# Pairing the x loads and grouping the stores of an eight-expert MLP, with fifteen small reads issued by SP

## The chip, the cores and the metric

The kernel runs on one core of a Trainium2 chip. The metric is the device time of one execution in microseconds (us); the kernel before was run five times, with a median of 184.09 us (183.85 to 184.23). A sixth execution was taken by the hardware profiler, and all durations below come from it.

## The reference

Eight experts each apply a two-layer MLP to their own 256 rows. All inputs and the output are float32.

```python
n_experts, capacity, hidden, expert_hidden = 8, 256, 512, 2048
# x: (8, 256, 512)   w1: (8, 512, 2048)   w2: (8, 2048, 512)
h = np.matmul(x, w1)
h = np.maximum(h, 0)
return np.matmul(h, w2).astype(np.float32)
```

One w1 and one w2 of an expert are 4 MB each in memory, one x is 512 KB and one output 512 KB. Everything together is 71.3 MB read and 4.2 MB written.

## The kernel before, in words

The loads cast from float32 to bfloat16 on the way, so they are all issued by POOL (`load_x`, line 66; `load_w1`, line 70; `load_w2`, line 74); only the x of experts 0 and 1 comes through SP in float32 and is cast by DVE (`load_x_first`, line 60). POOL also issues the stores of experts 0 to 6 (`store`, line 84). The last expert's two output halves are stored by SP and ACT (lines 160 to 162).

Per expert e: `prepare` (line 104) transposes x on PE through PSUM and DVE copies it to `xT`. `layer1` (line 117) makes `hT`, 64 matmuls of 256 columns with a Relu on ACT after every eight. `layer2` (line 139) makes the output, 32 matmuls of 512 columns into two PSUM banks, which DVE copies to `out_sb` (for the last expert, ACT copies the second half).

The order of PE's and POOL's instructions is the order in which the program writes them (`tc.manual_schedule`, line 166). POOL's order is that of `loads` (lines 89 to 94): for each expert x, w1, w2, with w1 of expert 7 ahead of w2 of expert 6. In iteration e of the main loop `issue` (line 96) takes from that list what may be issued by then (line 173), and `store(e - 1)` follows (line 175). The stores of experts 4, 5 and 6 (`DEFER`, line 56) are issued after the loop, behind all the loads.

w2 is loaded whole for experts 0 to 5, in three pieces of 8, 4 and 4 row blocks for expert 6, and in seven pieces of 4, 4, 3, 2, 1, 1, 1 for expert 7 (`PIECES`, line 53). A row block is 128 rows of w2: 256 KB in memory, and two matmuls of `layer2`. For the two experts with pieces `layer2` goes through the blocks in the outer loop, so that it can begin with the first piece.

POOL issues 37 transfers: 8 of w1, 16 of w2, 6 of x, 7 stores. Their completion semaphores go round: in the trace each transfer of POOL carries the semaphore of the one eight places earlier, and waits until that one has landed. So at most eight are in flight. Besides, a load waits for its buffer: w1 has four buffers, the whole w2 three, x four.

Of the kernel before, what the change touches and what calls it, by code (L numbers as in the profile page):

```python
# [9 lines left out]
FP32 = mybir.dt.float32  # L10
BF16 = mybir.dt.bfloat16


@with_exitstack
def kernel(
    ctx: ExitStack,
    tc: tile.TileContext,
    x: bass.AP,
    w1: bass.AP,
    w2: bass.AP,  # L20
    out: bass.AP,
):
    nc = tc.nc
    P = 128
    E, C, H = x.shape
    F = w1.shape[2]
    MC = C // P
    K1 = H // P
    K2 = F // P

    x_v = x.rearrange("e (p mo) k -> e p (mo k)", mo=MC)
    out_v = out.rearrange("e (p mo) k -> e p (mo k)", mo=MC)
    w1_v = w1.rearrange("e (p ko) n -> e p (ko n)", ko=K1)
    w2_v = w2.rearrange("e (p j) n -> e p (j n)", p=P)

    const = ctx.enter_context(tc.tile_pool(name="const", bufs=1))
    x_pool = ctx.enter_context(tc.tile_pool(name="x_pool", bufs=2))
    xb_pool = ctx.enter_context(tc.tile_pool(name="xb_pool", bufs=4))  # L40
    xT_pool = ctx.enter_context(tc.tile_pool(name="xT_pool", bufs=2))
    w1_pool = ctx.enter_context(tc.tile_pool(name="w1_pool", bufs=4))
    w2_pool = ctx.enter_context(tc.tile_pool(name="w2_pool", bufs=1))
    hT_pool = ctx.enter_context(tc.tile_pool(name="hT_pool", bufs=2))
    out_pool = ctx.enter_context(tc.tile_pool(name="out_pool", bufs=5))
    psum_t = ctx.enter_context(tc.tile_pool(name="psum_t", bufs=1, space=bass.MemoryType.PSUM))
    psum_h = ctx.enter_context(tc.tile_pool(name="psum_h", bufs=3, space=bass.MemoryType.PSUM))
    psum_o = ctx.enter_context(tc.tile_pool(name="psum_o", bufs=4, space=bass.MemoryType.PSUM))

    identity = const.tile([P, P], BF16, name="identity")  # L50


    PIECES = {E - 2: [8, 4, 4], E - 1: [4, 4, 3, 2, 1, 1, 1]}
    BUFS = {16: 3, 8: 1, 4: 4, 3: 1, 2: 1, 1: 3}

    DEFER = (E - 4, E - 3, E - 2)

    xbs, w1s, w2s, outs = {}, {}, {}, {}

    def load_x_first(e):  # L60
        t = x_pool.tile([P, MC * H], FP32, name="x_sb")
        nc.sync.dma_start(t[:], x_v[e])
        xbs[e] = xb_pool.tile([P, MC, P, K1], BF16, name="xb")
        nc.vector.tensor_copy(xbs[e][:].rearrange("p m q k -> p (m q k)"), t[:])  # L64

    def load_x(e):
        xbs[e] = xb_pool.tile([P, MC, P, K1], BF16, name="xb")
        nc.gpsimd.dma_start(xbs[e][:].rearrange("p m q k -> p (m q k)"), x_v[e])  # L68

    def load_w1(e):  # L70
        w1s[e] = w1_pool.tile([P, K1 * F], BF16, name="w1_sb")
        nc.gpsimd.dma_start(w1s[e][:], w1_v[e])  # L72

    def load_w2(e):
        w2s[e] = []
        k = 0
        for n in PIECES.get(e, [16]):
            c = w2_pool.tile([P, n * H], BF16, name=f"w2_{n}", bufs=BUFS[n])
            nc.gpsimd.dma_start(c[:], w2_v[e, :, k * H:(k + n) * H])  # L79
            for q in range(n):  # L80
                w2s[e].append(c[:, q * H:(q + 1) * H])
            k += n

    def store(e):
        nc.gpsimd.dma_start(out_v[e], outs[e][:].rearrange("p m h -> p (m h)"))  # L85

    loads = []
    for e in range(E):  # L90
        if e + 1 < E and e >= 1:
            loads.append((load_x, e + 1))
        loads += [(load_w1, e), (load_w2, e)]
    loads[-3], loads[-2] = loads[-2], loads[-3]

    def issue(upto):
        while loads:
            f, e = loads[0]
            if (f, e) not in upto:
                break  # L100
            loads.pop(0)
            f(e)

    def prepare(e):
        xb = xbs[e]
        xt_ps = psum_t.tile([P, K1, MC, P], BF16, name="xt_ps")
        for ko in range(K1):
            for mo in range(MC):
                nc.tensor.transpose(xt_ps[:, ko, mo, :], xb[:, mo, :, ko], identity[:])  # L109
        xT = xT_pool.tile([P, K1, C], BF16, name="xT")  # L110
        nc.vector.tensor_copy(  # L111
            xT[:].rearrange("p k c -> p (k c)"),
            xt_ps[:].rearrange("p k m q -> p (k m q)"),
        )
        return xT

    def layer1(e, xT):
        w1_r = w1s[e][:].rearrange("p (ko q j) -> p ko q j", ko=K1, j=K2)
        hT = hT_pool.tile([P, K2, C], BF16, name="hT")
        for pr in range(K2 // 2):  # L120
            h_ps = psum_h.tile([P, 2, C], FP32, name="h_ps")
            for s in range(2):
                j = pr * 2 + s
                for ko in range(K1):
                    nc.tensor.matmul(  # L125
                        h_ps[:, s, :],
                        w1_r[:, ko, :, j],
                        xT[:, ko, :],
                        start=(ko == 0),
                        stop=(ko == K1 - 1),  # L130
                    )
            nc.scalar.activation(  # L132
                hT[:, pr * 2:pr * 2 + 2, :].rearrange("p a c -> p (a c)"),
                h_ps[:].rearrange("p a c -> p (a c)"),
                mybir.ActivationFunctionType.Relu,
            )
        return hT

    def layer2(e, hT):
        last = e == E - 1  # L140
        out_sb = outs[e] = out_pool.tile([P, MC, H], FP32, name="out_sb")
        o_ps = [psum_o.tile([P, H], FP32, name="o_ps") for _ in range(MC)]
        if e in PIECES:
            order = [(k, m) for k in range(K2) for m in range(MC)]
        else:
            order = [(k, m) for m in range(MC) for k in range(K2)]
        for k, m in order:
            nc.tensor.matmul(  # L148
                o_ps[m][:],
                hT[:, k, m * P:(m + 1) * P],  # L150
                w2s[e][k],
                start=(k == 0),
                stop=(k == K2 - 1),
            )
            if k == K2 - 1:
                if last and m == 1:
                    nc.scalar.copy(out_sb[:, m, :], o_ps[m][:])  # L157
                else:
                    nc.vector.tensor_copy(out_sb[:, m, :], o_ps[m][:])  # L159
                if last:  # L160
                    eng = nc.scalar if m == 1 else nc.sync
                    eng.dma_start(out_v[e, :, m * H:(m + 1) * H], out_sb[:, m, :])

    load_x_first(0)
    load_x_first(1)
    with tc.manual_schedule(engines={mybir.EngineType.PE, mybir.EngineType.Pool}):
        f, e = loads.pop(0)
        f(e)
        make_identity(nc, identity)
        issue([(load_w2, 0), (load_x, 2), (load_w1, 1), (load_w2, 1), (load_x, 3), (load_w1, 2)])  # L170
        xT = prepare(0)
        for e in range(E - 1):
            issue([(load_w2, e + 2), (load_x, e + 4), (load_w1, e + 3), (load_w1, E - 1), (load_w2, e + 1)])
            if e > 0 and e - 1 not in DEFER:
                store(e - 1)
            hT = layer1(e, xT)
            xT = prepare(e + 1)
            if e == E - 2:
                hT_last = layer1(E - 1, xT)
            layer2(e, hT)  # L180
        for e in DEFER:
            store(e)
        layer2(E - 1, hT_last)


# [1 line left out]
_INS = ['x', 'w1', 'w2']  # L187
_OUTS = [((8, 256, 512), 'float32')]
# [25 lines left out]
```

## Time and profile before

| what | value |
|---|---|
| median of five runs | 184.09 us |
| the profiled execution, its own time | 183.88 us |
| its span, from the first to the last instruction | 182.1 us |
| PE busy | 128.3 us (70%) |
| POOL busy, 43 instructions | 20.8 us (11%) |
| POOL's transfers (queue q0), share of the 16 DMA engines' time | 97.6% |
| SP's and ACT's transfers (q1, q10) | 1.9% and 0.4% |
| HBM read and written | 71.30 MB and 4.19 MB |

A row of a timeline has the start and the duration in us, the engine, the line, the operation, what it writes and reads, and in brackets how long the engine had been idle and what ended that. "POOL" with an operation DMA_DIRECT2D is POOL writing the descriptors of one transfer; the transfer itself runs later on the 16 DMA engines. "Landing" is the moment when all 16 engines have raised the transfer's semaphore.

### The profile page before, as it was taken

To read this page: it belongs to the slowest core of one execution; us is meant where nothing else is said; L and a number is where in the kernel's file an instruction comes from. 1 tells how busy PE (TensorE), PEld (TensorE's weight loads), DVE (VectorE), ACT (ScalarE), POOL (GpSimd) and SP (SyncE) were. 2 spreads that over 40 slices of the span, in tenths; PEclk is the share of its full clock that TensorE was granted. 3 is DMA by queue.
4 is the path that set the end of the run, shared out by engine and by line. 5 is a ranking of instruction groups with operands and counts; after the bars stand their busy time and mean duration, and the time that the engine had idled before them with its cause. 6 is when DMAs were issued, how large, how long until landed. Compare 5 with 4: busy or idle time off the path is not lost.

```text
span 182.1 us, 1879 instructions
## 1 busy us (share of the span) xinstructions
PE 128.3 (70%) x832; PEld 90.1 (49%) x832; DVE 17.1 (9%) x25; ACT 40.1 (22%) x66; POOL 20.8 (11%) x43
## 2 busy tenths in 40 slices
PE   0205999296864959299880996929986498999860
PEld 0104884096324934079430892327942397964320
DVE  1200011101020011100130001200012001001110
ACT  2000450055001620026100360003600054630010
POOL 7401010110201011010200202011020101122200
PEclk9999999999999999969999699965999889999995
DMA  7999999999999999999999999999999999999993
GB/s 257 200 230 209 194 230 230 205 205 201 249 209 205 223 227 209 205 223 202 238 205 219 231 206 237 198 281 230 200 206 227 230 214 250 208 252 231 206 357 151
DMA packets 5911, 40.48 MB, mean 222 GB/s; under 512 B 656, under 2 KB 1040, under 8 KB 3984
## 3 DMA queue, kind: packets, MB, share of 16 engines
q0 software_dynamic: 5328, 38.80, 97.6%
q1 hardware_dynamic: 432, 1.31, 1.9%
q10 hardware_dynamic: 144, 0.26, 0.4%
q8 instruction: 6, 0.10, 0.2%
q14 instruction: 1, 0.01, 0.0%
HBM read 71.30 MB, written 4.19 MB: 415 GB/s over the span
## 4 chain that ended last, share of the span: by engine, by line
DMA 62%; another core or an unknown queue 25%; POOL 4%; PE 3%; issue 3%; ACT 0%; POOLq 0%
DMA w_sb<-in_w_dram 24%; DMA xb<-in_x_dram 23%; DMA w<-in_w_dram 15%; PE o_ps L148 3%; POOL w L79 1%; POOL xb L68 1%; POOL w_sb L72 1%; POOL out_dram L85 1%; ACT out_sb L157 0%; POOL identity masks.py:199 0%; POOL identity masks.py:197 0%; POOLq L79 0%; POOLq L85 0%; POOLq L198 0%
## 5 line engine op out<-in xcount | busy, mean ns | idle before, releaser
L125 PE MATMUL h_ps<-xT,w_sb 128*128 128x256 bf16 x512 | 67.4, 300 | 35.2 <-DMA w_sb<-in_w_dram 34.3
L125 PEld LDWEIGHTS <-w_sb 128*128 128x128 bf16 x512 | 61.1, 148 | 43.0 <-DMA w_sb<-in_w_dram 38.6
L132 ACT ACTIVATE hT<-h_ps 128x512 bf16<-128x512 f32 x64 | 38.2, 597 | 121.4 <-PE h_ps L125 121.4
L148 PE MATMUL o_ps<-w,hT 128*128 128x512 bf16 x256 | 57.0, 379 | 8.0 <-DMA w<-in_w_dram 7.8
L148 PEld LDWEIGHTS <-hT 128*128 128x128 bf16 x256 | 25.0, 98 | 37.8 <-issue 9.7
L159 DVE COPY out_sb<-o_ps 128x512 f32<-128x512 f32 x15 | 10.3, 691 | 62.2 <-PE o_ps L148 62.2
L79 POOL DMA_DIRECT2D w<-in_w_dram x16 | 8.7, 541 | 63.2 <-DMA w_sb<-in_w_dram 36.7
L111 DVE COPY xT<-xt_ps 128x1024 bf16<-128x1024 bf16 x8 | 5.5, 690 | 92.8 <-PE xt_ps L109 92.8
L109 PE MATMUL xt_ps<-identity,xb 128*128 128x128 bf16 x64 | 5.3, 231 | 4.7 <-DVE xb L64 4.7
L72 POOL DMA_DIRECT2D w_sb<-in_w_dram x8 | 4.6, 575 | 30.7 <-DMA w<-in_w_dram 17.8
L85 POOL DMA_DIRECT2D out_dram<-out_sb x7 | 3.7, 536 | 34.0 <-DMA w<-in_w_dram 11.2
L109 PEld LDWEIGHTS <-xb 128*128 128x128 bf16 x64 | 4.7, 117 | 4.7 <-DVE xb L64 4.7
L68 POOL DMA_DIRECT2D xb<-in_x_dram x6 | 3.2, 533 | 22.5 <-DMA w_sb<-in_w_dram 13.1
L157 ACT COPY out_sb<-o_ps 128x512 f32<-128x512 f32 x1 | 0.6, 585 | 14.6 <-PE o_ps L148 14.6
L64 DVE CAST xb<-x_sb 128x1024 bf16<-128x1024 f32 x2 | 1.4, 694 | 4.5 <-DMA x_sb<-in_x_dram 4.5
L132 ACT ACT_TABLE_LOAD x1 | 1.3, 1283 | 0.7 <-PEq L198 0.7
masks.py:199 POOL TENSOR_SCALAR_AFFINE_SELECT identity<-identity 128x128 bf16<-128x128 bf16 x1 | 0.3, 287 | 0.1
masks.py:197 POOL MEMSET identity<- 128x128 bf16 x1 | 0.2, 224 | 0.0
L198 POOL MEMSET const-float32-0.0<- 128x1 f32 x1 | 0.1, 100 | 0.2 <-issue 0.2
L198 POOL MEMSET const-bfloat16-1.0<- 128x1 bf16 x1 | 0.1, 101 | 0.0
L198 POOL MEMSET const-uint8-127<- 128x1 uint8 x1 | 0.1, 101 | 0.0
L198 POOL MEMSET const-float32-1.0<- 128x1 f32 x1 | 0.1, 98 | 0.0
## 6 DMA issues: line engine op xcount, KB each, us to landing
w_sb<-in_w_dram POOLq DMA_DIRECT2D x8, 2048.0 KB, 51.7
w<-in_w_dram POOLq DMA_DIRECT2D x6, 2048.0 KB, 48.8
out_dram<-out_sb POOLq DMA_DIRECT2D x7, 512.0 KB, 32.4
w<-in_w_dram POOLq DMA_DIRECT2D x4, 512.0 KB, 36.8
xb<-in_x_dram POOLq DMA_DIRECT2D x6, 256.0 KB, 44.8
x_sb<-in_x_dram SPq DMA_DIRECT2D x2, 512.0 KB, 3.6
w<-in_w_dram POOLq DMA_DIRECT2D x1, 1024.0 KB, 47.1
w<-in_w_dram POOLq DMA_DIRECT2D x1, 384.0 KB, 18.8
```

The source lines that it names most:

```text
L64: nc.vector.tensor_copy(xbs[e][:].rearrange("p m q k -> p (m q k)"), t[:])
L68: nc.gpsimd.dma_start(xbs[e][:].rearrange("p m q k -> p (m q k)"), x_v[e])
L72: nc.gpsimd.dma_start(w1s[e][:], w1_v[e])
L79: nc.gpsimd.dma_start(c[:], w2_v[e, :, k * H:(k + n) * H])
L85: nc.gpsimd.dma_start(out_v[e], outs[e][:].rearrange("p m h -> p (m h)"))
L109: nc.tensor.transpose(xt_ps[:, ko, mo, :], xb[:, mo, :, ko], identity[:])
L111: nc.vector.tensor_copy(xT[:].rearrange("p k c -> p (k c)"), xt_ps[:].rearrange("p k m q -> p (k m q)"),)
L125: nc.tensor.matmul(h_ps[:, s, :], w1_r[:, ko, :, j], xT[:, ko, :], start=(ko == 0), stop=(ko == K1 - 1),)
L132: nc.scalar.activation(hT[:, pr * 2:pr * 2 + 2, :].rearrange("p a c -> p (a c)"), h_ps[:].rearrange("p a c -> p (a c)"), mybir.ActivationF ...
L148: nc.tensor.matmul(o_ps[m][:], hT[:, k, m * P:(m + 1) * P], w2s[e][k], start=(k == 0), stop=(k == K2 - 1),)
L157: nc.scalar.copy(out_sb[:, m, :], o_ps[m][:])
L159: nc.vector.tensor_copy(out_sb[:, m, :], o_ps[m][:])
```

## The change

Six things are changed at once.

- **x** of experts 2 to 7 is loaded in three pairs instead of six singles.
- **Stores** of POOL go in three groups, experts (0, 1), (2, 3) and (4, 5, 6), instead of seven singles. Each group has an output tile of its own.
- **w2** has four whole buffers for all experts. The pieces are 8, 8 for expert 6 and 4, 4, 4, 2, 2 for expert 7.
- **`make_identity`** is called a second time. w2 of expert 0 is issued by its own call between the two; its place in POOL's order is as before.
- **`small_loads`** is called after `layer2(4)`: DVE copies 16 rows of expert 4's output into a tile, and SP then issues 15 reads of x into it, of k rows by 8·k floats for k from 15 down to 1. Nothing reads that tile.
- The tests in the loop that say when a load or a store may be issued are written for pairs and groups.

```diff
+    xg_v = x.rearrange("e (p mo) k -> p e (mo k)", mo=MC)
+    og_v = out.rearrange("e (p mo) k -> p e (mo k)", mo=MC)
...
-    xb_pool = ctx.enter_context(tc.tile_pool(name="xb_pool", bufs=4))
+    xb_pool = ctx.enter_context(tc.tile_pool(name="xb_pool", bufs=2))
...
-    w2_pool = ctx.enter_context(tc.tile_pool(name="w2_pool", bufs=1))
+    w2_pool = ctx.enter_context(tc.tile_pool(name="w2_pool", bufs=4))
...
-    out_pool = ctx.enter_context(tc.tile_pool(name="out_pool", bufs=5))
+    out_pool = ctx.enter_context(tc.tile_pool(name="out_pool", bufs=1))
...
-    PIECES = {E - 2: [8, 4, 4], E - 1: [4, 4, 3, 2, 1, 1, 1]}
-    BUFS = {16: 3, 8: 1, 4: 4, 3: 1, 2: 1, 1: 3}
-    DEFER = (E - 4, E - 3, E - 2)
+    PIECES = {E - 2: [8, 8], E - 1: [4, 4, 4, 2, 2]}
+    GROUPS = [(0, 1), (2, 3), (4, 5, 6), (7,)]
+    GROUP = {e: g for g in GROUPS for e in g}
+    DEFER = GROUPS[-2]
+    X_GROUPS = [(2, 3), (4, 5), (6, 7)]
...
-    def load_x(e):
-        xbs[e] = xb_pool.tile([P, MC, P, K1], BF16, name="xb")
-        nc.gpsimd.dma_start(xbs[e][:].rearrange("p m q k -> p (m q k)"), x_v[e])
+    def load_x(g):
+        t = xb_pool.tile([P, 2, MC, P, K1], BF16, name="xb2")
+        nc.gpsimd.dma_start(
+            t[:].rearrange("p e m q k -> p e (m q k)"), xg_v[:, g[0]:g[0] + 2, :]
+        )
+        for i, e in enumerate(g):
+            xbs[e] = t[:, i]
...
     def load_w2(e):
-        w2s[e] = []
+        w2s[e] = t = w2_pool.tile([P, K2 * H], BF16, name="w2_sb")
         k = 0
-        for n in PIECES.get(e, [16]):
-            c = w2_pool.tile([P, n * H], BF16, name=f"w2_{n}", bufs=BUFS[n])
-            nc.gpsimd.dma_start(c[:], w2_v[e, :, k * H:(k + n) * H])
-            for q in range(n):
-                w2s[e].append(c[:, q * H:(q + 1) * H])
+        for n in PIECES.get(e, [K2]):
+            nc.gpsimd.dma_start(t[:, k * H:(k + n) * H], w2_v[e, :, k * H:(k + n) * H])
             k += n
 
-    def store(e):
-        nc.gpsimd.dma_start(out_v[e], outs[e][:].rearrange("p m h -> p (m h)"))
+    def store(g):
+        nc.gpsimd.dma_start(
+            og_v[:, g[0]:g[-1] + 1, :], outs[g][:].rearrange("p e m h -> p e (m h)")
+        )
...
-        out_sb = outs[e] = out_pool.tile([P, MC, H], FP32, name="out_sb")
+        g = GROUP[e]
+        if e == g[0]:
+            outs[g] = out_pool.tile([P, len(g), MC, H], FP32, name=f"out_sb{g[0]}")
+        out_sb = outs[g][:, e - g[0]]
...
+    def small_loads(e):
+        probe = x_pool.tile([P, MC * H], FP32, name="x_sb")
+        nc.vector.tensor_copy(
+            probe[:16], outs[GROUP[e]][:16, e - GROUP[e][0]].rearrange("p m h -> p (m h)")
+        )
+        at = 0
+        for k in range(15, 0, -1):
+            nc.sync.dma_start(probe[:k, at:at + 8 * k], x[0, :k, :8 * k])
+            at += 8 * k
...
         make_identity(nc, identity)
-        issue([(load_w2, 0), (load_x, 2), (load_w1, 1), (load_w2, 1), (load_x, 3), (load_w1, 2)])
+        f, e = loads.pop(0)
+        f(e)
+        make_identity(nc, identity)
+        issue([(load_w2, 0), (load_x, X_GROUPS[0]), (load_w1, 1), (load_w2, 1), (load_w1, 2)])
...
-            issue([(load_w2, e + 2), (load_x, e + 4), (load_w1, e + 3), (load_w1, E - 1), (load_w2, e + 1)])
-            if e > 0 and e - 1 not in DEFER:
-                store(e - 1)
+            issue(
+                [(load_w2, e + 2), (load_w1, e + 3), (load_w1, E - 1), (load_w2, e + 1)]
+                + [(load_x, g) for g in X_GROUPS if g[0] <= e + 4]
+            )
+            for g in GROUPS[:-2]:
+                if g[-1] == e - 1:
+                    store(g)
...
             layer2(e, hT)
-        for e in DEFER:
-            store(e)
+            if e == 4:
+                small_loads(e)
+        store(DEFER)
         layer2(E - 1, hT_last)
```

## The prediction, made before the changed kernel was built or run

> **What bounds the kernel.** I read the page's DMA rows first, because PE is busy for only 70% of the span.
>
> ```profile
> span 182.1 us, 1879 instructions
> PE 128.3 (70%) x832; PEld 90.1 (49%) x832; DVE 17.1 (9%) x25; ACT 40.1 (22%) x66; POOL 20.8 (11%) x43
> ...
> DMA  7999999999999999999999999999999999999993
> ...
> DMA packets 5911, 40.48 MB, mean 222 GB/s; under 512 B 656, under 2 KB 1040, under 8 KB 3984
> ...
> q0 software_dynamic: 5328, 38.80, 97.6%
> ```
>
> The DMA engines are full from the second slice to the last but one, nearly all of it POOL's own transfers. In float32 the core moves 75.5 MB in 182 us, 415 GB/s. So the question is what the change does to the DMA engines' work, and at the two ends of that stream. The second view is POOL's timeline. Each row there starts when the transfer eight places earlier has landed, so the rows pace the stream:
>
> ```profile
> 143.81 0.53 POOL L79 DMA_DIRECT2D w<-in_w_dram  x1 [9.16 <-DMA w_sb<-in_w_dram]
> 153.53 0.53 POOL L79 DMA_DIRECT2D w<-in_w_dram  x1 [9.19 <-DMA w_sb<-in_w_dram]
> 154.79 0.53 POOL L79 DMA_DIRECT2D w<-in_w_dram  x1 [0.73 <-DMA out_dram<-out_sb]
> 159.61 0.53 POOL L79 DMA_DIRECT2D w<-in_w_dram  x1 [4.30 <-DMA w<-in_w_dram]
> 162.06 0.53 POOL L79 DMA_DIRECT2D w<-in_w_dram  x1 [1.92 <-DMA w<-in_w_dram]
> 164.56 0.53 POOL L79 DMA_DIRECT2D w<-in_w_dram  x1 [1.97 <-DMA w<-in_w_dram]
> 166.11 0.54 POOL L85 DMA_DIRECT2D out_dram<-out_sb  x1 [1.03 <-DMA out_dram<-out_sb]
> 168.51 0.54 POOL L85 DMA_DIRECT2D out_dram<-out_sb  x1 [1.86 <-DVE out_sb L159]
> 170.94 0.53 POOL L85 DMA_DIRECT2D out_dram<-out_sb  x1 [1.90 <-DMA w<-in_w_dram]
> ```
>
> A 4 MB w1 takes 153.53 - 143.81 = 9.72 us, a 512 KB store 154.79 - 153.53 = 1.26, a 1 MB piece 2.45 and 2.50. Transfers follow each other without a gap, and each is issued some 10 to 50 us before it lands. The third view is the end, by PE's timeline and SP's waits:
>
> ```profile
> 160.80 9.07 PE L148 MATMUL o_ps<-w,hT 128*128 128x512 bf16 x40
> 170.44 5.69 PE L148 MATMUL o_ps<-w,hT 128*128 128x512 bf16 x24 [0.57 <-DMA w<-in_w_dram]
> ```
>
> ```profile
> SPq L162 <- DVE out_sb L159: 175.1, 1, 175.1
> SPq L209 <- DMA out_dram<-out_sb: 3.2, 3, 2.2
> ```
>
> By the completion marks in the trace the last piece of w2 lands at 175.50, the deferred stores at 176.77, 178.00 and 179.26, the last expert's halves (issued at 176.67 and 176.78) at 179.91 and 180.55; the span ends 1.55 us later. The end is thus the end of the stream: 2 MB of stores after the last load, not PE.
>
> The 16 marks of one transfer are not equal. From 166 us on, one engine is last, six are 0.28 to 0.5 us ahead of it, and nine 1.25 to 1.8 us. The differences were made by single events (an instruction fetch of 16 KB takes 0.89 to 0.98 us of one engine, six times in the trace) and then stay, so all engines run at one rate. **The end is set by the most loaded engine**; work added to one of the nine is free up to 1.25 us.
>
> **Fewer transfers.** The bytes and nearly all descriptors stay; 37 transfers of POOL become 27 (x 6 to 3, stores 7 to 3, pieces of w2 10 to 7). Price of one transfer: expert 7's w2 takes 9.96 us in seven pieces (165.54 to 175.50), a whole one 9.70 (marks, mean of the undisturbed ones), so six more transfers cost 0.26, or 0.043 each. An x or a store, at 1.25 us, is 0.045 over two row blocks of 9.65/16 = 0.603. Ten at 0.045: **-0.45 us** on every engine.
>
> Here the Trainium skill states another price: "DMA: Bandwidth & Descriptors", section "Anatomy of one DMA — SWDGE (gpsimd) path", gives each transfer a fixed cost of about 2.0 us. By that rule ten fewer would bring 20 us. The row decides: a completion that nobody waits for lies beside the next transfer, and what is left of it is 0.045.
>
> **POOL's issues.** Ten less, 10 x 0.53 = 5.3 us of POOL, and the second identity costs it 0.22 + 0.29 = 0.51 us at 3 us into the span. Cost nothing: POOL is idle for 89%, and the issues behind the identity (x pair, w1, w2) are for transfers that run after 25.5 us. PE needs the identity at 4.68; it is then written again until about 3.1.
>
> **Waits for buffers and places.** With 27 transfers in a rotation of eight I followed each: the first eight go out in the first iteration, later ones wait for the eighth before or for a buffer. The latest against its turn are the x pair (6, 7), which waits for `prepare(3)` (DVE's copy at 64.84 now, about 1.3 later with the pair ahead), turn at about 108; and the group (4, 5, 6), which waits for `layer2(6)` (PE until 167.9, copies until 168.98), turn at 175.1. The four w2 buffers ask for `layer2(3)`, over at about 96, before expert 7's w2, turn at 164. No turn is missed; the margin is at least 6 us. If it were gone, each us late is one us of end. The pair puts 1.25 us before some w1, which delays PE by as much, and PE idles for 30%; the order of bytes before the last load is the same at the end.
>
> **PE at the end.** After the last load four matmuls remain instead of two, and the piece before it has four too. With 0.237 us each (5.69/24): from the landing T of the last load, the third piece of four (landed T - 2.5) is done at T - 0.6, the next four at T + 0.3, the last four at T + 1.3 (now T + 0.63). The stores of SP and ACT are then issued at about T + 1.8 and 1.9, 0.65 us later. On the last engine POOL's stores run until T + 3.4, and the first packets of SP's last store came 0.85 after its issue, T + 2.7 in the new kernel. **Cost 0**, cover 0.7 us; beyond it each us counts.
>
> **The small loads.** DVE's copy of 16 rows (nearest row: 128x1024, 0.69 us) stands behind `layer2(4)`'s copies at about 116 us; the next of DVE is 13 us later. Cost 0. SP is empty between 1.6 and 176.7 us; 15 issues of 0.35 are 5.3 us, hidden, if they get done.
>
> On the engines they are 120 descriptors of 32 to 480 B and up to 120 completion marks: 15 of each on one engine, down to one on another, none on a sixteenth. The trace before has no such descriptor. Bounds, by its DMA records of SP's queue: a mark takes 9 ns, 2048 B 84 ns, so 75 ns per 2 KB above the mark. Low end: 0, when the last engine is the sixteenth or the added work fits in the 0.28 us by which others are ahead. Interpolated: 9 + size/27.3 ns and 9 for the mark; the fullest engine 15 x 18 ns + 3840 B/27.3 = 0.41, the mean over 16 engines (120 x 18 ns + 39.7 KB/27.3)/16 = 0.23. High end: each like the 2 KB row with a POOL mark of 22: 15 x 0.106 = 1.6 on the fullest, 0.8 on the mean. I can't see which engine is last, so I take the mean of the interpolation, nearest in size to the mark, and 0.02 for an engine that overtakes: **+0.25**.
>
> A rule of the same page speaks against this part: "Rules for kernel authors" says to coalesce, under 64 KB one pays mostly overhead, and its "Measured" table has 0.68 us for 4 KB. 15 x 0.68 = 10 us, if they ran alone. No row here shows that a small transfer holds up another queue: the fetches of instructions cut into POOL's 9.7 us transfers and cost the engine just their own 0.9. So it bears on SP's wait, not on the sum.
>
> **Sum**, against the profiled execution: 183.88 - 0.45 + 0.25 = 183.68, or 0.20 less; at the median's level 184.09 - 0.20 = **183.9 us**. Its own range is 183.5 to 184.3.
>
> **Rivals.**
> 1. *The small loads are free* (20%). The last engine has few of them. For: nine engines of sixteen have 1.25 us to give, and the fullest price, 0.41, exceeds the 0.28 lead of the next six by little. Against: nothing says where the last engine stands in the row. Time: 184.09 - 0.45 = 183.64.
> 2. *A small descriptor costs as much as a 2 KB one or more* (15%). For: the skill's page says in "Specifications" that below 512 B the engine does a read-modify-write, and no run here shows its price. Against: the 9 ns mark is small too. Time: 184.09 - 0.45 + 0.8 = 184.4, up to 185.2 on the fullest engine.
> 3. *SP's queue starves behind POOL's* (13%), slower. For: at the start POOL's first packets began when SP's two x loads were out, and at the end on the seven later engines SP's packets began just when POOL's were out; the two did not mix. Then the small loads, issued at 117, would wait for the end of POOL's stream, about 178.8; if SP goes round eight semaphores as POOL does, its ninth issue waits for the first landing, seven more take 7 x 0.35 = 2.5, and SP's last store goes out at 181.3 and lands some 2 us later, at 183.3, where 180.55 ended before: +2.75, 186.8. It decides from the point where the seventh small load (whose place the fifteenth takes) lands after 174. Against: instruction fetches do cut into POOL's stream, and at the end POOL's last transfer had begun before SP's reached most of the engines, so that the trace can't tell starving from taking turns.
>
> A fourth, that the grouping lets the engines run dry, has no place in the waits followed above.
>
> **How the numbers follow.** A measurement of this kernel can tell about 0.2%, 0.37 us, from no change. The forecast has 50%: with an uncertainty of 0.25, 12 of it faster, 38 the same. Free: 16 faster, 4 the same. Dear: 12 slower, 3 the same. Starved: 13 slower. The last 2% are unnamed, split. Faster 0.29, the same 0.45, slower 0.26. The range goes from 183.4 (free, with the scatter of the runs) to 185.3 (dear, fullest engine) and leaves the starved case out.
>
> **What would show it.** POOL has 27 transfers; expert 7's w2 takes 9.87 us (five pieces); the last load lands 0.35 earlier, corrected for the small loads; the end follows the last load by 6.6 us still. The 15 small reads land well before 170 (the forecast), or at the end (rival 3: SP's waits for landings of its own reads, and a DMA row with idle engines in the last slice). The spread of the 16 marks before and after 120 us gives the price of small descriptors. The forecast is wrong if the last load comes no earlier, or if the time after it grows.

## The result, and the profile after

The changed kernel takes 183.59 us (median of 27 runs, 183.12 to 184.56) against 184.11 for the kernel before (46 runs): a ratio of 0.9972, 95% interval 0.9962 to 0.9982, or 0.5 us faster (0.3 to 0.7). A second set on another occasion gave 0.9963 (0.9948 to 0.9978). The range held it; the forecast of 183.9 was 0.3 too high, and the likeliest case had been "no change that can be told". The profiled execution of the changed kernel took 183.34 us.

Lines of the page after (span; busy times by engine; share of the 16 DMA engines by queue):

```profile
span 181.3 us, 1882 instructions
...
PE 126.8 (70%) x832; PEld 88.8 (49%) x832; DVE 17.8 (10%) x26; ACT 40.1 (22%) x66; POOL 17.0 (9%) x35
...
q0 software_dynamic: 4784, 38.80, 97.4%
q1 hardware_dynamic: 672, 1.35, 2.1%
```

The core is bound as before: POOL's queue fills the DMA engines, PE is idle for 30%. SP's queue q1 has 240 packets more, 120 descriptors and 120 completion marks; before it had:

```profile
q1 hardware_dynamic: 432, 1.31, 1.9%
```

POOL's timeline at the end:

```profile
124.12 0.53 POOL L88 DMA_DIRECT2D w_sb<-in_w_dram  x1 [1.76 <-DMA out_dram<-out_sb]
134.09 0.53 POOL L88 DMA_DIRECT2D w_sb<-in_w_dram  x1 [9.44 <-DMA w_sb<-in_w_dram]
143.57 0.53 POOL L88 DMA_DIRECT2D w_sb<-in_w_dram  x1 [8.95 <-DMA w_sb<-in_w_dram]
153.27 0.53 POOL L88 DMA_DIRECT2D w_sb<-in_w_dram  x1 [9.17 <-DMA w_sb<-in_w_dram]
168.56 0.75 POOL L92 DMA_DIRECT2D out_dram<-out_sb  x1 [14.76 <-DVE out_sb L172]
```

The last loads are all issued by 153.8, eleven us earlier than before, and the group of stores at 168.56, with its turn at 175.1; no turn is missed. PE's end and SP's queue:

```profile
170.16 1.89 PE L161 MATMUL o_ps<-w_sb,hT 128*128 128x512 bf16 x8 [0.56 <-DMA w_sb<-in_w_dram]
172.62 3.61 PE L161 MATMUL o_ps<-w_sb,hT 128*128 128x512 bf16 x16 [0.57 <-DMA w_sb<-in_w_dram]
```

```profile
0.74 0.85 SPq L67 DMA_DIRECT2D x_sb<-in_x_dram  x2
117.40 20.84 SPq L185 DMA_DIRECT2D x_sb<-in_x_dram  x15
176.77 0.38 SPq L175 DMA_DIRECT2D out_dram<-out_sb  x1
```

PE is done at 176.2, 1.1 us after the last load landed (175.09), and SP issues its 15 reads from 117.4 to 138.2; their last mark is at 151.8. SP's queue is not starved. While POOL loads w2 in descriptors that read 32 KB of float32 each, the engines give SP one descriptor or mark after each of POOL's (a pace of 1.23 us). During POOL's store ahead of that, in descriptors of 4 KB, SP got nothing for most of the time: by the DMA records the store's first descriptor starts at 119.21, SP's first at 121.24, and the earliest engine is through with the store at 121.72.

Where the 0.78 us between the two spans (182.10 and 181.32) came from, by the completion marks (the 16 engines each raise one when their part of a transfer is done):

| stretch | before | after | difference |
|---|---|---|---|
| mean of the 16 engines' marks of the last load | 174.46 | 174.09 | -0.37 |
| last engine behind that mean | 1.04 | 1.00 | -0.04 |
| last load to the last store's landing | 5.05 | 5.03 | -0.02 |
| last landing to the end | 1.55 | 1.20 | -0.35 |

Not all of that is in the device time, which is the metric. The device time is 1.78 us longer than the span before and 2.02 us after, and so it stays in all runs of the two kernels (1.73 to 1.85, and 1.96 to 2.08). So 0.24 us of the 0.78 is given back outside the span, where the profile shows nothing: the two profiled executions are 0.54 us apart (183.88 and 183.34), and the medians 0.5.

The last row of the table was not in the prediction. SP's waits at the end, before and after (L209 and L239 are the same place; the row named PEq is the barrier of all engines):

```profile
SPq L209 <- PEq L209: 1.3, 2, 1.0
```

```profile
SPq L239 <- DMA out_dram<-out_sb: 2.8, 2, 2.2
...
SPq L239 <- PEq L239: 0.6, 2, 0.5
```

In the barrier SP waits for POOL: before, POOL stands still from 181.26 to 181.67 between two of its own last rows, and it doesn't after. The first row of the table hides a second thing. In the kernel before all 16 engines stall together at 94.5 to 98.1 us, in w1 of expert 4 (`layer1(4)` begins at 99.89, when it has landed): its descriptors take up to 2.31 us for 1.23, and the transfer takes 10.97 us for 9.70. I had seen that transfer and left it out as disturbed. It is no accident: the changed kernel has its stall at 116.4 to 119.6, in w1 of expert 5, and the second set of runs has it there again. By the sum of what the descriptors took too long it costs the mean engine 0.86 us before and 0.53 after. Marks "without the stall" are, from here on, the mean mark less this sum. A stretch of each trace (length, busy us of PE, PEld, DVE, ACT, POOL with counts, clock, DMA share, GB/s), before, then after:

```profile
91.00:94.00 3.00, 3.00 (x16) 1.35 (x15) 0.69 (x1) 0.00 (x0) 0.00 (x0) 1.00 1.02 218
94.00:97.00 3.00, 0.73 (x4) 0.12 (x2) 0.69 (x1) 0.00 (x0) 0.00 (x0) 1.00 1.08 175
```

```profile
116.00:119.00 3.00, 0.00 (x0) 0.00 (x0) 1.34 (x2) 0.00 (x0) 0.00 (x0) 1.00 0.99 175
```

The engines count as busy, but move 175 GB/s; in the stretch just before the first stall they moved 218.

### The profile page after: what moved, and what is told of

The parts are those of the page before. It is cut to its first block, busy times and chain, and to the rows that moved or that the text cites. A ratio compares the mean times of both kernels' runs of the same rounds, so it can differ in the third digit from the quotient of the medians.

```text
span 181.3 us, 1882 instructions
## 1 busy us (share of the span) xinstructions
PE 126.8 (70%) x832; PEld 88.8 (49%) x832; DVE 17.8 (10%) x26; ACT 40.1 (22%) x66; POOL 17.0 (9%) x35
## 3 DMA queue, kind: packets, MB, share of 16 engines
q1 hardware_dynamic: 672, 1.35, 2.1%
## 4 chain that ended last, share of the span: by engine, by line
DMA 70%; another core or an unknown queue 12%; PE 10%; POOL 3%; issue 2%; ACT 0%; POOLq 0%
DMA w_sb<-in_w_dram 45%; DMA xb<-in_x_dram 25%; PE o_ps L161 6%; PE h_ps L135 4%; POOL w_sb L82 1%; POOL w_sb L88 1%; POOL out_dram L92 0%; POOL xb L74 0%; ACT out_sb L170 0%; POOL identity masks.py:199 0%; POOL identity masks.py:197 0%; PE xt_ps L119 0%; POOLq masks.py:199 0%; POOLq L88 0%
## 5 line engine op out<-in xcount | busy, mean ns | idle before, releaser
L135 PE MATMUL h_ps<-xT,w_sb 128*128 128x256 bf16 x512 | 64.2, 291 | 34.0 <-DMA w_sb<-in_w_dram 33.2
L135 PEld LDWEIGHTS <-w_sb 128*128 128x128 bf16 x512 | 59.3, 147 | 40.4 <-DMA w_sb<-in_w_dram 37.3
L161 PE MATMUL o_ps<-w_sb,hT 128*128 128x512 bf16 x256 | 58.5, 387 | 10.7 <-DMA w_sb<-in_w_dram 10.7
L88 POOL DMA_DIRECT2D w_sb<-in_w_dram x13 | 6.9, 534 | 78.4 <-DMA w_sb<-in_w_dram 75.1
L82 POOL DMA_DIRECT2D w_sb<-in_w_dram x8 | 4.7, 590 | 29.7 <-DMA w_sb<-in_w_dram 26.6
L74 POOL DMA_DIRECT2D xb<-in_x_dram x3 | 2.1, 716 | 26.4 <-PE xt_ps L119 26.4
L92 POOL DMA_DIRECT2D out_dram<-out_sb x3 | 2.2, 727 | 17.5 <-DVE out_sb L172 14.8
L180 DVE COPY x_sb<-out_sb 16x1024 f32<-16x1024 f32 x1 | 0.7, 680 | 0.0
```

The costliest lines, as they stand in the source:

```text
L74: nc.gpsimd.dma_start(t[:].rearrange("p e m q k -> p e (m q k)"), xg_v[:, g[0]:g[0] + 2, :])
L88: nc.gpsimd.dma_start(t[:, k * H:(k + n) * H], w2_v[e, :, k * H:(k + n) * H])
L92: nc.gpsimd.dma_start(og_v[:, g[0]:g[-1] + 1, :], outs[g][:].rearrange("p e m h -> p e (m h)"))
L135: nc.tensor.matmul(h_ps[:, s, :], w1_r[:, ko, :, j], xT[:, ko, :], start=(ko == 0), stop=(ko == K1 - 1),)
L161: nc.tensor.matmul(o_ps[m][:], hT[:, k, m * P:(m + 1) * P], w2s[e][:, k * H:(k + 1) * H], start=(k == 0), stop=(k == K2 - 1),)
L180: nc.vector.tensor_copy(probe[:16], outs[GROUP[e]][:16, e - GROUP[e][0]].rearrange("p m h -> p (m h)"))
```

## The experiments

Theory A is the prediction with small reads that fall where the last engine doesn't feel them; B keeps their 0.25 us and gives the rest of the change more. C to G came up on the way. "Run 2" below is the changed kernel without the small reads. The runs were made on four occasions, on which the kernel before took 184.02 to 184.10; each ratio is against the kernel before on the same occasion.

**1. The changed kernel again**, unedited.

> The changed kernel once more, as the yardstick on the same chip as the runs beside it. Both theories: about 0.5 us under the kernel before (0.9972 of it), 183.6.

183.45 us, 0.9963 (0.9948 to 0.9978).

**2. Without the small reads.**

```diff
-            if e == 4:
-                small_loads(e)
```

> The changed kernel without the fifteen small reads and without DVE's copy into their tile; all else as changed. Theory A (a transfer saved brings 0.045 us, the small reads fall where the last DMA engine doesn't feel them): 0.45 to 0.5 us under the kernel before, the same as the changed kernel within 0.1 us. Theory B (the small reads cost the 0.25 us of the prediction, and the rest of the change brings about 0.75): 0.75 us under the kernel before, 0.25 under the changed kernel.

183.18 us, 0.9946 (0.9925 to 0.9966): 0.27 under the changed kernel beside it, though the two intervals overlap. By the marks, the mean of the last load without the stall is 173.34 (174.01 less 0.67), against 173.56 (174.09 less 0.53) with them: +0.22.

**3. The small reads alone, on the kernel before**, with the function as in the change (its `outs` by expert):

```diff
             layer2(e, hT)
+            if e == 4:
+                small_loads(e)
```

> The kernel before with the fifteen small reads alone added after the fifth expert. Theory A: within 0.1 us of the kernel before. Theory B: 0.25 us slower.

184.35 us, 1.0011 (0.9996 to 1.0026): +0.30, with an interval that just takes in zero. Together with run 2 this speaks for B, though neither difference is clear of noise alone: the small reads cost about what the prediction gave them, and something else brings more.

**4. More transfers.** Each w1 and each whole w2 in halves, without small reads:

```diff
-        nc.gpsimd.dma_start(w1s[e][:], w1_v[e])
+        h = K1 * F // 2
+        for i in range(2):
+            nc.gpsimd.dma_start(w1s[e][:, i * h:(i + 1) * h], w1_v[e, :, i * h:(i + 1) * h])
...
-        for n in PIECES.get(e, [K2]):
+        for n in PIECES.get(e, [8, 8]):
```

> The changed kernel without the small reads, and each w1 and each whole w2 loaded in two halves: 14 more transfers, the same bytes. Theory A: 14 x 0.045 = 0.63 us slower than the same kernel without the halves. If the gain of the change does not come from the number of transfers (theory C: from the new order of x and stores, or from the pieces at the end): no slower, within 0.1 us. By a fixed cost of 2 us each: 28 us slower.

183.51 us, 0.9975 (0.9964 to 0.9985): +0.33 over run 2, between A and C. The trace takes it apart: the mean mark of the last load is where it was (174.02), but the stall is gone (0.03 us for 0.67), so 14 transfers cost 173.99 - 173.34 = 0.65 on the mean engine, 0.046 each. The last landing is 180.03 (180.20 in run 2), and the end follows it by 1.68 us (0.86), of which 0.25 comes back outside the span (device time less span is 1.76 for 2.02).

**5. A longer program on POOL.** Without small reads, 16 memsets of a spare tile after its first transfers:

```diff
+        for _ in range(16):
+            nc.gpsimd.memset(spare[:], 0.0)
         xT = prepare(0)
```

> The changed kernel without the small reads, with 16 memsets of a spare tile added on POOL behind its first eight transfers; no DMA is changed, and the memsets (0.1 us each by the rows of POOL's other memsets) fall into POOL's first long wait. Theory D (part of the gain is POOL's shorter program: at the end of the program POOL's own last steps take 1.55 us after the last landing in the kernel before, which has 12 more rows on POOL, and 0.86 without the small reads): the time from the last landing to the end grows by 0.3 to 0.8 us and the whole with it. Theory E (the end after the last landing has nothing to do with the length of POOL's program): the same as without the memsets, within 0.1 us.

182.94 us, 0.9943 (0.9929 to 0.9957), and 0.98 us from the last landing to the end. Theory D falls: these memsets do not make the pause. E said the same time within 0.1 us, and the median is 0.24 under run 2's; the span is not shorter (181.2 us for 181.1), the part outside the span is (1.76 us for 2.02).

**6. The price of a small descriptor**, by 40 reads on all 16 engines:

```diff
-        at = 0
-        for k in range(15, 0, -1):
-            nc.sync.dma_start(probe[:k, at:at + 8 * k], x[0, :k, :8 * k])
-            at += 8 * k
+        for k in range(40):
+            nc.sync.dma_start(probe[16 * (k % 7) + 16:16 * (k % 7) + 32,
+                120 * (k // 7 % 8):120 * (k // 7 % 8) + 120], x[0, :16, :120])
...
-            if e == 4:
+            if e == 0:
```

(DVE's copy into the tile takes all 128 rows here.)

> The changed kernel with 40 small reads of 16 rows by 120 floats after the first expert in place of the fifteen, so each of the 16 DMA engines gets 40 descriptors of 480 B and 40 marks (one engine got at most 15 of each in the change). By the interpolated price of the prediction (27 ns and 9 to 22 for the mark): 1.4 to 2.0 us over the kernel without small reads. If a small descriptor costs as much as 2 KB: 3.7 to 4.2 us. If small reads cost the engines nothing: no difference.

184.49 us, 1.0023 (1.0014 to 1.0032): 1.31 over run 2, and 1.55 over run 5, which was made beside it. The stall at 116 us is gone here too and a smaller one, 0.20, is at 64.7 to 69.2. Without stalls the mean mark of the last load is 175.34 - 0.20 = 175.14, 1.80 us later than in run 2, 0.045 us for a descriptor of 480 B and its mark. The interpolation (0.036 to 0.049) holds. In the change the mean engine pays 120 x 0.045/16 = 0.34 by this price, a little high since most of its reads are shorter; 0.22 was measured.

**7. Sixteen matmuls after the last load.** Pieces of expert 7, without small reads:

```diff
-    PIECES = {E - 2: [8, 8], E - 1: [4, 4, 4, 2, 2]}
+    PIECES = {E - 2: [8, 8], E - 1: [4, 4, 8]}
```

> The changed kernel without the small reads, with expert 7's w2 in pieces of 4, 4, 8 in place of 4, 4, 4, 2, 2: sixteen matmuls are left after the last load in place of four. By the prediction's account of the end (POOL's stores cover PE until 3.4 us after the last load): PE ends 3.8 us after it, SP's and ACT's first packets come at about 5.05, 1.65 later than the cover, less two transfers: 1.5 us slower than without the small reads. If PE's end is on the path already: 2.5 us slower. If the stores of the last expert hide more than that: no slower.

186.16 us, 1.0094 (1.0064 to 1.0123): 3.0 over run 2, twice the forecast. PE's timeline, and the stretch around its last matmuls:

```profile
170.31 1.89 PE L161 MATMUL o_ps<-w_sb,hT 128*128 128x512 bf16 x8 [0.55 <-DMA w_sb<-in_w_dram]
...
175.17 5.15 PE L161 MATMUL o_ps<-w_sb,hT 128*128 128x512 bf16 x16 [2.97 <-DMA w_sb<-in_w_dram]
...
180.86 0.35 SPq L175 DMA_DIRECT2D out_dram<-out_sb  x1
```

```profile
171.90:175.00 3.10, 0.30 (x2) 0.02 (x1) 0.00 (x0) 0.00 (x0) 0.00 (x0) 0.98 0.95 297
175.00:178.40 3.40, 3.23 (x8) 1.13 (x8) 0.00 (x0) 0.00 (x0) 0.00 (x0) 0.51 0.67 275
178.40:181.00 2.60, 1.92 (x9) 0.69 (x7) 0.69 (x1) 0.59 (x1) 0.00 (x0) 1.00 0.00 2
```

The account of the cover was right: POOL's stores ended on the last engine at 178.57, 3.44 after the load, and SP's first packet came at 181.71, 0.85 after its issue. But PE had been idle for 2.97 us, and its granted clock fell to half for the next 3.4: sixteen matmuls took 5.15 us for 3.8. That is the missing 1.35.

**8. x in pairs alone, on the kernel before** (one execution): `load_x` as in the change, two buffers, and the loop's list with pairs.

```diff
-        if e + 1 < E and e >= 1:
+        if e in (1, 3, 5):
...
-        issue([(load_w2, 0), (load_x, 2), (load_w1, 1), (load_w2, 1), (load_x, 3), (load_w1, 2)])
+        issue([(load_w2, 0), (load_x, 2), (load_w1, 1), (load_w2, 1), (load_w1, 2)])
```

> The kernel before with x in pairs alone (34 transfers of POOL for 37). One look, for two things. By the price per transfer the mean of the 16 marks of the last load comes 0.13 us earlier. The stall of all engines at once, which the kernel before has at 94.5 us (0.86 us) and the changed one at 116.4 (0.5): if it moves with the order of POOL's transfers, it is elsewhere than at 94.5 here; if it belongs to stores or pieces, it stays.

183.66 us. The stall stays at 94.5 (0.82 us): it does not go with x. Without it the last load's mean mark is 173.49 for 173.60, -0.11 for three transfers.

In all kernels so far that have the stall, the transfer in which it falls is the one just ahead of the first store in POOL's queue: w1 of expert 4 before, w1 of expert 5 after. That is theory F (runs 9, 10 and 12; where run 10's expectation says w1 of expert 3, POOL's order has that of expert 4).

**9. All stores last.** Without small reads and second identity; x and w1 as in the change:

```diff
-    PIECES = {E - 2: [8, 8], E - 1: [4, 4, 4, 2, 2]}
+    PIECES = {E - 1: [8, 8]}
-    GROUPS = [(0, 1), (2, 3), (4, 5, 6), (7,)]
+    GROUPS = [(0, 1, 2, 3, 4, 5), (6,), (7,)]
```

> The changed kernel without the small reads and without the second identity, with all stores of POOL behind the last load (experts 0 to 5 in one, expert 6 in one), w2 of expert 6 whole and of expert 7 in two halves: 22 transfers for 27. Theory F (all engines stall in the load just ahead of the first store in POOL's queue): no stall between 20 us and the last load; with five transfers less at 0.045 and the stall of 0.5 to 0.67 us gone, 182.2 to 182.5, about 0.7 under the kernel without small reads. Theory G (the stall has nothing to do with the stores): a stall of 0.5 or more is there somewhere, and the time is 182.8 to 182.9. PE's end is later (sixteen matmuls after the last load) but 3.5 MB of stores cover it for 8 us.

181.71 us, 0.9874 (0.9853 to 0.9895): faster than both kernels and than F had said. Between 110 and 165 us there is no stall, and 0.11 us of one at 165.5, in the last load, now the one ahead of the first store. The stretch at 116 us, and the end of POOL's timeline:

```profile
116.00:119.00 3.00, 0.00 (x0) 0.00 (x0) 0.07 (x1) 0.00 (x0) 0.00 (x0) 1.00 1.13 240
```

```profile
108.51 0.53 POOL L88 DMA_DIRECT2D w_sb<-in_w_dram  x1 [8.91 <-DMA w_sb<-in_w_dram]
138.97 0.84 POOL L92 DMA_DIRECT2D out_dram<-out_sb  x1 [29.93 <-DVE out_sb L172]
167.33 0.55 POOL L92 DMA_DIRECT2D out_dram<-out_sb  x1 [27.51 <-DVE out_sb L172]
```

The last landing is at 178.96, 1.24 us earlier than in run 2: 0.56 by the stall, about 0.2 by five transfers less; most of the rest is the last engine, 0.60 behind the mean at the last of POOL's stores (1.16 in run 2). The two stores that SP and ACT issue at 173.8 get their first packet at 176.14, when POOL's are nearly out on the first engines, and are the last to land; they were issued early enough that PE's end is covered.

**10. The first store early.** Without small reads; one execution.

```diff
-    GROUPS = [(0, 1), (2, 3), (4, 5, 6), (7,)]
+    GROUPS = [(0,), (1,), (2, 3), (4, 5, 6), (7,)]
```

> The changed kernel without the small reads, with the stores of experts 0 and 1 apart, so that the first store stands behind w1 of expert 3, as in the kernel before, and not behind w1 of expert 5. One look. Theory F: the stall is at 94 to 98 us, in w1 of expert 3, as in the kernel before, and not at 116 us. Theory G: it stays at 116.4 us.

```profile
94.00:97.00 3.00, 2.24 (x11) 0.80 (x9) 0.69 (x1) 0.00 (x0) 0.00 (x0) 1.00 1.11 175
...
116.00:119.00 3.00, 3.00 (x15) 1.37 (x14) 0.69 (x1) 0.00 (x0) 0.00 (x0) 1.00 1.07 229
```

The stall is back at 94.5 us with 0.87, and gone from 116. F holds for the place, G falls. It isn't PE's pause either: PE is busy for 2.24 us of that stretch here, and for 0.73 before. (183.41 us.)

**11. Twelve tiny transfers on POOL** (1 KB each, two an iteration), without small reads; one execution.

```diff
+            if e < 6:
+                for k in (2 * e, 2 * e + 1):
+                    nc.gpsimd.dma_start(spare[:16, 16 * k:16 * k + 16], x[0, :16, :16])
```

> The changed kernel without the small reads, with twelve transfers of 1 KB added on POOL, two an iteration, nothing reads them: 39 transfers of POOL. One look, at the time from the last landing to the end: 1.55 to 1.72 us in the three kernels with 37 to 41 transfers, 0.86 to 1.20 in those with 34 or fewer. If the number of POOL's transfers makes it: 1.5 to 1.7. If not: 0.9 to 1.2. The added descriptors cost each engine up to 12 x 0.05 = 0.6 us besides.

1.62 us from the last landing to the end, as forecast from the number of transfers. Its price on the way: the last load's mean mark without the stall is 173.54, so 12 transfers of 1 KB cost 0.2, 0.017 each. (183.41 us.)

**12. All stores last and nothing else**, against run 2.

```diff
-    GROUPS = [(0, 1), (2, 3), (4, 5, 6), (7,)]
+    GROUPS = [(0, 1, 2, 3, 4, 5), (6,), (7,)]
```

> The changed kernel without the small reads, with all stores of POOL behind the last load and nothing else changed (pieces and both identities as in the changed kernel): 26 transfers for 27. Theory F: no stall ahead of the last load or a small one, so 0.5 to 1.1 us under the kernel without small reads (0.56 on the mean of the engines, and up to 0.4 more on the last one, which the stall set back further than the mean): 182.0 to 182.6. If the gain of the variant with late stores came from its fewer pieces of w2 instead: 182.9 to 183.1.

182.87 us, 0.9928 (0.9903 to 0.9952): 0.3 under run 2, less than forecast, and with intervals that overlap. The trace has no stall at all. The stretch in w1 of expert 5, in run 2 and here:

```profile
116.00:119.00 3.00, 0.00 (x0) 0.00 (x0) 0.10 (x1) 0.00 (x0) 0.00 (x0) 1.00 1.03 175
```

```profile
116.00:119.00 3.00, 0.03 (x1) 0.00 (x0) 0.69 (x1) 0.00 (x0) 0.00 (x0) 1.00 1.08 229
```

The last landing is 0.98 earlier than in run 2 (179.22 for 180.20), as F says. But the end follows it by 1.86 us:

```profile
SPq L237 <- DMA out_dram<-out_sb: 7.0, 1, 7.0
SPq L237 <- PEq L237: 1.4, 2, 1.0
```

SP signals at 179.53, POOL answers at 180.37. With 26 transfers this takes run 11's reading away: POOL's pause at the end is not made by the number of its transfers either.

## Why the prediction was near, and where it was off

**What bounds the kernel** held in every run: what lengthened the stream of the DMA engines lengthened the kernel, and PE mattered only when it outran its cover (run 7).

**Fewer transfers, -0.45.** The term was too large. To the last load eight transfers less brought 0.26 us without the stall (173.60 before, 173.34 in run 2), 0.033 each; the two after it brought nothing that shows (5.05 and 5.04 us). The runs put a split load at 0.046, x pairs at 0.037, a tiny transfer at 0.017. The price was taken from expert 7's pieces, where it is 0.043, and laid on everything.

**The small loads, +0.25.** Right, as far as the noise lets one tell: +0.22 by the marks, +0.27 and +0.30 by the medians of runs 2 and 3, and the price of one by run 6. Rival 2 (dear) falls by run 6, rival 3 (SP starved) by the trace after. Against rival 1 (free) stand three estimates that agree, none of them clear of zero alone.

**PE's end, cost 0, and the places in the queue** held: SP issued its last store 1.68 us after the last load (1.8 said), and the stores ended by the stream. The second identity was written until 3.58 us, not 3.1, still ahead of PE's first need at 4.80.

**What the sum lacked: a term for two things that the trace of before already held.** One is the stall ahead of the first store, set aside as disturbance; with the stores grouped it moved and was smaller, -0.33 on the mean engine. The other is the time after the last landing, of which the prediction said that the end would follow the last load "by 6.6 us still"; it followed by 6.2, since POOL no longer pauses (-0.35), and the part outside the span took 0.24 of that back. With measured sizes, in the profiled executions: -0.26 - 0.33 + 0.22 for the mean mark of the last load, -0.04 - 0.02 - 0.35 from there, and + 0.24 outside the span, make -0.54; the forecast had -0.20. These sizes come from one trace of each kernel.

So the account of what bounds the kernel and of the small loads was right, and the size was off: the gain was two and a half times the forecast. That it still came near, and within the range, is in part luck. The transfers were credited with 0.19 too much, which made up for more than half of the stall that was left out.

What stays open: why the engines stall there. That it comes with the first store is shown by runs 10 and 12, which change nothing but the stores' groups and with them their places (run 9 agrees); the mechanism is not shown, nor why grouping makes it smaller. In runs 4 and 6 the first store follows w1 of expert 5 and there is hardly a stall; in run 4 the load ahead has shorter rows, which also holds for runs 9 and 12, but in run 6 it has not. Open too is what makes POOL pause at the end: 37 to 41 transfers went with it in four kernels, but so did 26 in run 12, and nothing was tried that removes it alone. And open is the part of the device time outside the span, about 1.8 us in some of the kernels and 2.0 to 2.2 in others.

## What to carry to other kernels

When DMA engines are full, price a change by what it adds to the engines' streams, and look at each transfer that took longer than its bytes before calling it noise: one that is in the trace of a second execution at the same place belongs to the kernel. Stores that nobody waits for are worth trying behind the last load, where they also cover the end of the computation: together with fewer pieces of w2 and one identity less that took 1.5 us off run 2's time (run 9), and alone 0.3 us, which is not clear of noise (run 12). Small transfers cost by the number of their descriptors and marks on each engine, hundredths of a us each, and not by the latency that each has alone. And a gain read inside the span has to be looked for in the device time: here 0.24 of 0.78 us did not arrive there.

## What the runs showed of the hardware that was not expected

- All 16 DMA engines stall together, for 0.5 to 0.9 us, in the load ahead of the first store of POOL's queue; the store was issued 43 to 63 us before it landed. It is so in all the traces here but those of runs 4, 6, 9 and 12, where that load has 0.11 us of it at most.
- A read issued by SP beside a full queue of POOL is served one descriptor at a time after each of POOL's 32 KB descriptors (1.23 us), so that a read of one descriptor an engine takes two turns, 2.45 us; of a store of POOL's with 4 KB descriptors, 2.5 us on an engine, the first 2.0 passed before SP was served at all.
- One descriptor of 480 B and its mark cost an engine 0.045 us in a full stream.
- After 2.97 us without work PE's granted clock was 0.5 for 3.4 us (run 7). The Trainium skill, "TensorE: Matmul & The Clock Gate", section "Part 1: The HAM clock gate (the "warmup" mystery)", gives a window of about 3.4 us for both ways; the time at half clock agrees, while the pause that led to it was shorter, 2.97 us.
- The last steps of the program, after the last landing, took from 0.86 to 1.86 us in kernels whose rows there are nearly the same; the device time was longer than the span by 1.8 us in some kernels and by 2.0 to 2.2 in others.
